# One mLSTM layer on one core: weight buffers of one alignment, SiLU as one function, conv taps on ScalarE, Newton steps on GpSimd

## The chip, the cores and the metric

The kernel runs on one core of a Trainium2 chip. The metric is device time in microseconds (us). Three runs of the kernel before took 1791.73, 1795.51 and 1797.22 us, so the median is 1795.51. PE is the matrix engine (TensorE), DVE is VectorE, ACT is ScalarE, POOL is GpSimd, and SP only issues DMA transfers.

## The reference, cut to what matters

All numbers are float32. There is one layer, with 256 tokens and a width of 4096:

```python
h = rms_norm(x, norm_w)
u = h @ w_in                                  # 4096 -> 2048 q, 2048 k, 4096 v, 4096 og, 4096 z, 16 gates
qk = silu(causal_dwconv(qk, conv_w, conv_b))  # four taps per channel
# for each of 8 heads (q, k of 256, v of 512), tokens in chunks: weights from the gates,
# num = (a * (q @ k.T)) @ v + state terms;  hc = num / max(|qn|, exp(-m))
hn = hc * rsqrt(mean(hc * hc) + EPS) * out_norm_w
y = hn * sigmoid(og) * silu(z)
out = x + y @ w_out
```

## The kernel before

**Products.** Every large product is made of float32 values split into a rounded high half and the rest, the low half (`split`: ACT copies the high half, L135, DVE subtracts to get the low one, L136). `matmul3` then issues three matmuls: high by high, high by low, low by high (L140 to L142). The left operand (128 x 128, activations turned) is the stationary one; a weight block of 128 x 512 moves through.

**Projections.** `project_pair` computes two column blocks of 512 for all 256 tokens. There are 15 pairs over x (`oz0`, `qkv1`, `oz1`, ... `oz7`) and 4 over y (`o0` to `o3`). The 4096 rows are eight chunks. Chunks 0, 2, 4 and 6 (`FAST`) use seven products P1 to P7 in place of eight, for which DVE adds weight blocks (`prepare`, L281: `w<-w,w`); the others use four plain steps. Each step takes one `operand`: a raw weight tile of 2 x 128 rows by 512 columns, kept as 128 x 1024, and its halves `wh` and `wl`. A fast step has 6 matmuls and a plain one 12. A pair has 28 fast and 16 plain steps, so 44 operands and 360 matmuls of 128 x 512; 19 pairs have 6840.

**Buffers.** `wh` and `wl` each rotate over four tiles (tags `whi`, `wlo` of `wpool`) of RAW = 1056 columns, since stage 1 needs that many: 4224 bytes in each partition, 16.5 times 256. So neighbouring tiles start alternately on a multiple of 256 bytes and 128 bytes past one. As 44 is a multiple of 4, a step has the same buffer in every pair. In the built program the four `wh` tiles start at 160640, 164864, 169088 and 173312, the four `wl` tiles follow in the same way; a `wh` tile and its `wl` tile are of one kind, and all left operands start 128 bytes past a multiple of 256.

**Stage 1** (L559 to L604, the first 110 us) needs no normalised x. For each half of a chunk it loads x turned (`xT`) and 1056 + 1024 weight columns (`wf`), scales x by `norm_w` on the fly into the halves `lhs` (L583 on ACT, L584 on DVE), and forms the gates and the q, k, v of head 0 (`first_P`). Beside it `row_squares` and `row_stats` form the rsqrt of each row (`rstd`, `rstdB`), and `build_x` scales x (`xn`, L250) and makes the left operands `lhs_x` of the projections, for chunks 0 to 4 in stage 1 and for 5 to 7 right behind it.

**Heads.** The work of a head sits in a deque, `queue`, of small functions that `pump` runs evenly between the steps of the pairs: `combine` (P1 to P7 out of PSUM), `conv_qk` (turn q or k, ACT's first tap L440, three more taps fused on DVE L447, SiLU as sigmoid L452 and product L453), `head` (weights, `num`, the sum of squares, and `scale`: rsqrt by a seed and three Newton steps on 128 x 2), `gate_1` (sigmoid of og and z, then DVE products L645 and L646), `finish` (y times its rsqrt times the gate, L519) and `turn` (y turned, scaled, spilled to DRAM, L541 and L544). At the end `build_y` loads the spilled chunks and makes `lhs_y`. The tile framework orders the instructions of each engine by a timeline simulation of its own; program order within an engine is then fixed.

```python
hi = wpool.tile([P, RAW], F32R, name=f"wh_{name}", tag="whi")[:, :n]   # L147
for it in range(3):                                                    # L128, rsqrt
    nc.vector.tensor_mul(t, r, r)
    nc.vector.scalar_tensor_tensor(t, t, -0.5, src, op0=OP.mult, op1=OP.mult)
    nc.vector.scalar_tensor_tensor(dst if it == 2 else r, t, 1.5, r, op0=OP.add, op1=OP.mult)
```

Of the kernel before, what the change touches and what calls it, by code (L numbers as in the profile page):

```python
# [11 lines left out]
F32 = mybir.dt.float32  # L12
# [3 lines left out]
OP = mybir.AluOpType  # L16
# [25 lines left out]
FAST = (0, 2, 4, 6)  # L42
# [20 lines left out]
def mlstm_layer(ctx: ExitStack, tc: tile.TileContext, x, xT, norm_w, w_first, w_in, conv_w, conv_b, gate_b,  # L63
# [4 lines left out]
    wpool = ctx.enter_context(tc.tile_pool(name="wpool", bufs=4))  # L68
    work = ctx.enter_context(tc.tile_pool(name="work", bufs=1))
# [51 lines left out]
    def rsqrt(dst, src, n, tag):  # L121

        r = small.tile([P, n], F32, name=f"rs_r_{tag}", tag=f"rs_r{n}", bufs=1)
        t = small.tile([P, n], F32, name=f"rs_t_{tag}", tag=f"rs_t{n}", bufs=1)
        i = small.tile([P, n], I32, name=f"rs_i_{tag}", tag=f"rs_i{n}", bufs=1)
        nc.vector.tensor_scalar(i, src.bitcast(I32), 1, None, op0=OP.logical_shift_right)
        nc.vector.tensor_scalar(r.bitcast(I32), i, -1.0, float(0x5F3759DF), op0=OP.mult, op1=OP.add)
        for it in range(3):  # L128
            nc.vector.tensor_mul(t, r, r)
            nc.vector.scalar_tensor_tensor(t, t, -0.5, src, op0=OP.mult, op1=OP.mult)  # L130
            nc.vector.scalar_tensor_tensor(dst if it == 2 else r, t, 1.5, r, op0=OP.add, op1=OP.mult)
# [12 lines left out]
    def operand(name, src):  # L144

        n = src.shape[-1]
        hi = wpool.tile([P, RAW], F32R, name=f"wh_{name}", tag="whi")[:, :n]  # L147
        lo = wpool.tile([P, RAW], F32R, name=f"wl_{name}", tag="wlo")[:, :n]
        split(hi, lo, src)
        return hi, lo  # L150
# [4 lines left out]
    def load(name, w, off, n):  # L155
        raw = wpool.tile([P, RAW], F32, name=f"w_{name}", tag="wraw", bufs=6)[:, :n]
        nc.sync.dma_start(raw, source(w, off, n))
        return raw
# [37 lines left out]
    def build(c, src, of):  # L196

        if c in FAST:
# [42 lines left out]
    def build_x(c):  # L241
        src = big(f"xn_{c}", [P, CK, T])

        def scaled(j0):
            def run():
                if j0 == 0:
                    nc.sync.dma_start(src, xT[:, c * CK:(c + 1) * CK, :])
                for j in range(j0, j0 + 2):
                    k = c * CK + j
                    nc.vector.scalar_tensor_tensor(src[:, j, :], src[:, j, :], nw[:, k:k + 1], rstdB,  # L250
                                                   op0=OP.mult, op1=OP.mult)
            return run
        return [scaled(0), scaled(2)] + lazy(lambda: build(c, src, "x"), 4 if c in FAST else 2)
# [63 lines left out]
    def project_pair(name, w, off, of, between=None):  # L317
        ps = {}
        plain = [u for c in range(NCH) if c not in FAST for u in plain_steps(name, w, off, c)]
        steps = []  # L320
        for c in FAST:
            for group in fast_steps(name, w, off, c):
                steps += group
                if plain:
                    steps.append(plain.pop(0))
        assert not plain
        uses = {s: len(FAST) * HK for s in TAGS}
        for s in ("P2", "P3", "P4", "P5"):
            uses[s] += (NCH - len(FAST)) * CK
        seen = dict.fromkeys(TAGS, 0)  # L330
        left = {c: 7 if c in FAST else 4 for c in range(NCH)}
# [93 lines left out]
    def conv_qk(h, u):  # L425

        def one(i):
# [27 lines left out]
            return [turned, taps(0), taps(1), silu, lambda: split(qk[i][0], qk[i][1], t_["acc"])]
# [71 lines left out]
    def turn(h):  # L527
# [18 lines left out]
        if h == HEADS - 1:  # L546
            out += lazy(lambda: build(h, yT[0], "y"), 4 if h in FAST else 2)
        return out

    def build_y(c):  # L550
# [5 lines left out]
        return [make] + lazy(lambda: build(c, src[0], "y"), 4 if c in FAST else 2)  # L556
# [4 lines left out]
    FW = GQ + DQK + DV  # L561
    for c in range(NCH):
# [4 lines left out]
        for k0 in range(0, CK, HK):  # L567
            parts = [(0, 1), (1, 2)] if c == 0 and k0 == 0 else [(0, HK)]
            for a, z in parts:
# [36 lines left out]

    u0 = work.tile([P, NT, NB], F32, name="u_0", tag="cA")
# [9 lines left out]
    hs, finish = head(0)  # L617
# [6 lines left out]
    for n, (what, h, _, _) in enumerate(pairs):  # L624
# [7 lines left out]
        if what == "qkv":  # L632
            hs, finish = head(h)
# [41 lines left out]
def blocks_of(w, s1, s2):  # L675
# [3 lines left out]
    for c in range(NCH):  # L679
        if c in FAST:  # L680
# [36 lines left out]
```

## Time and profile before

| | us |
|---|---|
| three runs, median | 1795.51 |
| the profiled execution, its own time | 1793.31 |
| its span in the profile | 1791.6 |
| PE busy | 1756.1 (98%) |
| DVE busy | 1655.5 (92%) |
| ACT busy | 1107.1 (62%) |
| POOL busy | 12.1 (1%) |

The granted clock of PE is 0.993 of full speed over the whole span. A page shows busy time by engine, what each engine waited for, and groups of instructions by source line. An engine that is busy most of the time need not be the one that ends last; the waits tell that. Matmuls overlap in the array: one lasts about 0.39 us in the profile, and the next starts some 0.23 us after it, so for PE the distance of starts counts and not the duration.

### The profile page before, as it was taken

What the parts mean: (1) busy time and instruction counts of PE and PEld (TensorE: products, weight loads), DVE (VectorE), ACT (ScalarE), POOL (GpSimd) and SP (SyncE); (2) the same over time, 40 slices, a digit from 0 to 9 for tenths busy, and PEclk for the clock granted to TensorE, in tenths of its full rate; (3) what the DMA queues carried; (4) which work ended last, traced back from release to release, by engine and by line L of the source; (5) the groups of instructions that cost most, each with busy time, mean ns of one, the idle gap of its engine ahead of it and who ended that gap; (6) DMA issues with size and microseconds to landing.
All of it is one profiled execution on the core that took longest, in us unless ns stands there. A gap on an engine that the chain in (4) does not pass through costs nothing.

```text
span 1791.6 us, 21695 instructions
## 1 busy us (share of the span) xinstructions
PE 1756.1 (98%) x7804; PEld 1419.5 (79%) x7804; DVE 1655.5 (92%) x1823; ACT 1107.1 (62%) x1271; POOL 12.1 (1%) x29
## 2 busy tenths in 40 slices
PE   9979999999999999999999999999999989999998
PEld 8867878888888788788878887888788768787876
DVE  5899999999999999989998999899999999989897
ACT  7566666665666666656666566566656666565654
POOL 0000000000000000000000000000000000000000
PEclk9999999999999999999999999999999989999999
DMA  9755565556555656565556566655555747767563
GB/s 368 262 167 193 171 221 191 193 190 219 192 192 179 217 182 202 174 234 188 188 192 218 188 193 205 208 186 195 202 193 183 234 154 258 244 212 241 195 221 121
DMA packets 107724, 365.67 MB, mean 204 GB/s; under 512 B 12128, under 2 KB 12512, under 8 KB 107616
## 3 DMA queue, kind: packets, MB, share of 16 engines
q1 hardware_dynamic: 105360, 356.95, 59.4%
q0 software_dynamic: 1968, 6.82, 1.0%
q8 instruction: 61, 1.00, 0.2%
q10 hardware_dynamic: 288, 0.52, 0.1%
q14 instruction: 47, 0.39, 0.1%
HBM read 356.38 MB, written 7.86 MB: 203 GB/s over the span
## 4 chain that ended last, share of the span: by engine, by line
PE 86%; DVE 7%; ACT 3%; issue 2%; DMA 1%; SPq 0%; DVEq 0%; ACTq 0%
PE P_oz L140 11%; PE P_oz L141 11%; PE P_oz L142 11%; PE P_qkv L141 10%; PE P_qkv L142 10%; PE P_qkv L140 10%; PE P_o L141 5%; PE P_o L142 5%; PE P_o L140 5%; ACT wh_qkv_P L135 1%; PE first_P L140 1%; PE first_P L141 1%; PE first_P L142 1%; DVE wl_oz_P L136 1%; DVE wl_oz L136 1%
## 5 line engine op out<-in xcount | busy, mean ns | idle before, releaser
L135 ACT ACTIVATE wh_oz_P<-w_oz 128x1024 fp32r<-128x1024 f32 x224 | 233.8, 1056 | 166.2 <-DVE w_oz L281 85.7
L136 DVE TENSOR_TENSOR wl_oz_P<-w_oz,wh_oz_P 128x1024 fp32r<-128x1024 f32 x224 | 269.0, 1216 | 19.5 <-ACT wh_oz_P L135 19.5
L135 ACT ACTIVATE wh_qkv_P<-w_qkv 128x1024 fp32r<-128x1024 f32 x196 | 206.4, 1060 | 114.3 <-PE P_qkv L142 77.6
L136 DVE TENSOR_TENSOR wl_qkv_P<-w_qkv,wh_qkv_P 128x1024 fp32r<-128x1024 f32 x196 | 236.8, 1220 | 29.8 <-ACT wh_qkv_P L135 28.7
L141 PE MATMUL P_oz<-wl_oz,lhs_x 128*128 128x512 f32 x512 | 202.7, 396 | 0.0
L142 PE MATMUL P_oz<-wh_oz,lhs_x 128*128 128x512 f32 x512 | 201.3, 393 | 0.0
L140 PE MATMUL P_oz<-wh_oz,lhs_x 128*128 128x512 f32 x512 | 195.2, 396 | 1.8 <-ACT wh_oz L135 0.9
L141 PE MATMUL P_oz<-wl_oz_P,lhs_x 128*128 128x512 f32 x448 | 179.0, 400 | 1.1 <-DVE wl_oz_P L136 1.1
L140 PE MATMUL P_oz<-wh_oz_P,lhs_x 128*128 128x512 f32 x448 | 175.9, 402 | 3.9 <-ACT wh_oz_P L135 3.8
L141 PE MATMUL P_qkv<-wl_qkv,lhs_x 128*128 128x512 f32 x448 | 177.4, 396 | 0.9 <-DVE wl_qkv L136 0.9
L142 PE MATMUL P_oz<-wh_oz_P,lhs_x 128*128 128x512 f32 x448 | 177.1, 395 | 0.0
L142 PE MATMUL P_qkv<-wh_qkv,lhs_x 128*128 128x512 f32 x448 | 176.1, 393 | 0.0
L135 ACT ACTIVATE wh_o_P<-w_o 128x1024 fp32r<-128x1024 f32 x112 | 117.6, 1059 | 93.5 <-PE P_o L142 53.1
L135 ACT ACTIVATE wh_qkv<-w_qkv 128x1024 fp32r<-128x1024 f32 x112 | 118.5, 1058 | 79.2 <-PE P_qkv L142 66.0
L140 PE MATMUL P_qkv<-wh_qkv,lhs_x 128*128 128x512 f32 x448 | 166.7, 393 | 0.0
L135 ACT ACTIVATE wh_oz<-w_oz 128x1024 fp32r<-128x1024 f32 x128 | 134.8, 1053 | 47.4 <-PE P_oz L142 22.5
L136 DVE TENSOR_TENSOR wl_oz<-w_oz,wh_oz 128x1024 fp32r<-128x1024 f32 x128 | 155.7, 1217 | 7.5 <-ACT wh_oz L135 7.3
L281 DVE TENSOR_TENSOR w_oz<-w_oz,w_oz 128x1024 f32<-128x1024 f32 x128 | 155.7, 1217 | 0.5
L141 PE MATMUL P_qkv<-wl_qkv_P,lhs_x 128*128 128x512 f32 x392 | 154.7, 395 | 0.0
L142 PE MATMUL P_qkv<-wh_qkv_P,lhs_x 128*128 128x512 f32 x392 | 154.2, 393 | 0.0
L136 DVE TENSOR_TENSOR wl_o_P<-w_o,wh_o_P 128x1024 fp32r<-128x1024 f32 x112 | 135.3, 1219 | 18.9 <-ACT wh_o_P L135 18.8
L140 PE MATMUL P_qkv<-wh_qkv_P,lhs_x 128*128 128x512 f32 x392 | 150.2, 398 | 1.1 <-ACT wh_qkv_P L135 1.0
(216 smaller groups left out, 3436.7 us busy)
## 6 DMA issues: line engine op xcount, KB each, us to landing
w_oz<-in_w_in SPq DMA_DIRECT2D x256, 512.0 KB, 4.3
w_qkv<-in_w_in SPq DMA_DIRECT2D x224, 512.0 KB, 4.3
w_o<-in_w_out SPq DMA_DIRECT2D x128, 512.0 KB, 4.4
wf<-in_w_first SPq DMA_DIRECT2D x15, 528.0 KB, 6.7
wf<-in_w_first SPq DMA_DIRECT2D x15, 512.0 KB, 6.7
xr<-in_x SPq DMA_DIRECT2D x8, 512.0 KB, 8.6
xn<-in_xT SPq DMA_DIRECT2D x8, 512.0 KB, 5.7
xo<-in_x SPq DMA_DIRECT2D x16, 256.0 KB, 5.2
```

What stands on the lines that cost most here:

```text
L135: nc.scalar.activation(hi, src, AF.Copy)
L136: nc.vector.tensor_sub(lo, src, hi.bitcast(F32))
L140: nc.tensor.matmul(ps, a[0], b[0], start=first, stop=False)
L141: nc.tensor.matmul(ps, a[0], b[1], start=False, stop=False)
L142: nc.tensor.matmul(ps, a[1], b[0], start=False, stop=last)
L281: nc.vector.tensor_add(raw[step[1]], raw[step[1]], raw[step[2]])
```

## The change

1. The `wh` and `wl` tiles have 1024 columns (4096 bytes), so all of them start at the same offset; in the built program this is 128 bytes past a multiple of 4096. Raw weights get a pool of their own (still 1056 columns). The 1056-column operands of stage 1 go to `wide_operand`: two pairs of work tiles, `v0`/`v1` and `cA`/`cB`, in turn. `V` moves to the tags `v0`/`v1`.
2. SiLU is one ACT function (`AF.Silu`), for the convolution and for z; the DVE product behind the sigmoid is gone. ACT loads its function tables 27 times in place of 19: `gate_1` now has two loads.
3. A tap of the convolution is a scaled copy on ACT for each of two blocks and one DVE addition over both.
4. A Newton step of `rsqrt` has four plain operations in place of three, two of them fused. The one of a head runs on GpSimd (with `ss`), except the two integer operations of its seed. The one of the rows stays on DVE.
5. `build_x`: four scalings by `norm_w` on ACT, then one DVE product of 128 x 1024 with `rstdB`.
6. Stage 1: x is scaled in place on ACT, and both blocks of a half chunk are split in one operation of 128 x 512 on each engine.
7. `FAST` becomes a dictionary with the same chunks for x and y; the plain steps are dealt out by a formula that gives the same order as before.

Instructions on each engine, before and after: DVE 1767 and 1618, ACT 1191 and 1273, POOL 34 and 138; PE and SP are equal.

```diff
-FAST = (0, 2, 4, 6)
+FAST = {"x": (0, 2, 4, 6), "y": (0, 2, 4, 6)}
     wpool = ctx.enter_context(tc.tile_pool(name="wpool", bufs=4))
+    rawpool = ctx.enter_context(tc.tile_pool(name="rawpool", bufs=6))
-    def rsqrt(dst, src, n, tag):
+    def rsqrt(dst, src, n, tag, eng=nc.vector):
...
-            nc.vector.tensor_mul(t, r, r)
-            nc.vector.scalar_tensor_tensor(t, t, -0.5, src, op0=OP.mult, op1=OP.mult)
-            nc.vector.scalar_tensor_tensor(dst if it == 2 else r, t, 1.5, r, op0=OP.add, op1=OP.mult)
+            eng.tensor_mul(t, r, r)
+            eng.tensor_mul(t, t, src)
+            eng.tensor_scalar(t, t, -0.5, 1.5, op0=OP.mult, op1=OP.add)
+            eng.tensor_mul(dst if it == 2 else r, t, r)

...
     def operand(name, src):

         n = src.shape[-1]
-        hi = wpool.tile([P, RAW], F32R, name=f"wh_{name}", tag="whi")[:, :n]
-        lo = wpool.tile([P, RAW], F32R, name=f"wl_{name}", tag="wlo")[:, :n]
+        hi = wpool.tile([P, HK * NB], F32R, name=f"wh_{name}", tag="whi")[:, :n]
+        lo = wpool.tile([P, HK * NB], F32R, name=f"wl_{name}", tag="wlo")[:, :n]
         split(hi, lo, src)
         return hi, lo

+    def wide_operand(name, src, n):
+
+        tags = (("v0", "v1"), ("cA", "cB"))[n % 2]
+        hi, lo = (work.tile([P, RAW], F32R, name=f"w{i}_{name}", tag=tag)[:, :src.shape[-1]]
+                  for i, tag in enumerate(tags))
+        split(hi, lo, src)
+        return hi, lo
+
     def source(w, off, n):
         return bass.AP(tensor=w.tensor, offset=w.offset + off, ap=[[n, P], [1, n]])

     def load(name, w, off, n):
-        raw = wpool.tile([P, RAW], F32, name=f"w_{name}", tag="wraw", bufs=6)[:, :n]
+        raw = rawpool.tile([P, RAW], F32, name=f"w_{name}", tag="wraw")[:, :n]
         nc.sync.dma_start(raw, source(w, off, n))
         return raw

...
     def build_x(c):
         src = big(f"xn_{c}", [P, CK, T])

-        def scaled(j0):
-            def run():
-                if j0 == 0:
-                    nc.sync.dma_start(src, xT[:, c * CK:(c + 1) * CK, :])
-                for j in range(j0, j0 + 2):
-                    k = c * CK + j
-                    nc.vector.scalar_tensor_tensor(src[:, j, :], src[:, j, :], nw[:, k:k + 1], rstdB,
-                                                   op0=OP.mult, op1=OP.mult)
-            return run
-        return [scaled(0), scaled(2)] + lazy(lambda: build(c, src, "x"), 4 if c in FAST else 2)
+        def scaled():
+            nc.sync.dma_start(src, xT[:, c * CK:(c + 1) * CK, :])
+            for j in range(CK):
+                nc.scalar.activation(src[:, j, :], src[:, j, :], AF.Copy, scale=nw[:, c * CK + j:c * CK + j + 1])
+            nc.vector.tensor_mul(src, src, rstdB.unsqueeze(1).to_broadcast([P, CK, T]))
...
         ps = {}
-        plain = [u for c in range(NCH) if c not in FAST for u in plain_steps(name, w, off, c)]
+        fast = FAST[of]
...
-                t_["acc"], t_["sg"] = both[:, 0], both[:, 1]
+                t_["acc"], t_["tp"] = both[:, 0], both[:, 1]
...
-            def taps(a):
+            def tap(j):
                 def run():
-                    acc, pt, ct = t_["acc"], t_["pt"], ct0 + a
-                    for j in range(1, CONV):
-                        nc.vector.scalar_tensor_tensor(acc[:, a, j:], pt[:, a, :T - j], cw[:, 3 - j, ct:ct + 1],
-                                                       acc[:, a, j:], op0=OP.mult, op1=OP.add)
+                    acc, tp, pt = t_["acc"], t_["tp"], t_["pt"]
+                    for a in range(2):
+                        nc.scalar.activation(tp[:, a, :T - j], pt[:, a, :T - j], AF.Copy,
+                                             scale=cw[:, 3 - j, ct0 + a:ct0 + a + 1])
+                    nc.vector.tensor_add(acc[:, :, j:], acc[:, :, j:], tp[:, :, :T - j])
                 return run

             def silu():
-                nc.scalar.activation(t_["sg"], t_["acc"], AF.Sigmoid)
-                nc.vector.tensor_mul(t_["acc"], t_["acc"], t_["sg"])
-
-            return [turned, taps(0), taps(1), silu, lambda: split(qk[i][0], qk[i][1], t_["acc"])]
+                nc.scalar.activation(t_["acc"], t_["acc"], AF.Silu)
+
+            return [turned, tap(1), tap(2), tap(3), silu, lambda: split(qk[i][0], qk[i][1], t_["acc"])]
         return one(0) + one(1)


-    V = [lhs_pool.tile([P, NT, DV], F32R, name=f"v{part}") for part in range(2)]
     y = {}

-    def head(h):
+    def head(h, V):

         qT, kT = qk
         A = [work.tile([P, 3 * P], F32R, name=f"A{part}_{h}", tag=f"A{part}") for part in range(2)]
...
         def scale():
-            nc.vector.tensor_scalar(ss, ss, 1.0 / DV, EPS, op0=OP.mult, op1=OP.add)
-            rsqrt(s2, ss, NT, f"h{h}")
+            nc.gpsimd.tensor_scalar(ss, ss, 1.0 / DV, EPS, op0=OP.mult, op1=OP.add)
+            rsqrt(s2, ss, NT, f"h{h}", nc.gpsimd)
...
                     ws.append(raw)
                 for k in range(k0 + a, k0 + z):
-                    s = nw[:, c * CK + k:c * CK + k + 1]
-                    nc.scalar.activation(xh[:, k, :], xraw[:, k, :], AF.Copy, scale=s)
-                    nc.vector.scalar_tensor_tensor(xl[:, k, :], xraw[:, k, :], s, xh[:, k, :].bitcast(F32),
-                                                   op0=OP.mult, op1=OP.subtract)
-                ops = [operand(f"f_{c}_{k0}_{a}_{i}", raw) for i, raw in enumerate(ws)]
+                    nc.scalar.activation(xraw[:, k, :], xraw[:, k, :], AF.Copy, scale=nw[:, c * CK + k:c * CK + k + 1])
+                split(xh[:, k0 + a:k0 + z, :], xl[:, k0 + a:k0 + z, :], xraw[:, k0 + a:k0 + z, :])
+                ops = [wide_operand(f"f_{c}_{k0}_{a}", ws[0], wides), operand(f"f_{c}_{k0}_{a}", ws[1])]
+                wides += 1
                 for k in range(n):
                     kk = k0 + a + k
                     for i, (o, wd, b) in enumerate(first):
...

+    V = [work.tile([P, RAW], F32R, name=f"v{part}", tag=f"v{part}")[:, :NT * DV].rearrange("p (t c) -> p t c", t=NT)
+         for part in range(2)]
     u0 = work.tile([P, NT, NB], F32, name="u_0", tag="cA")
...
         else:
-            sg = {}
-
-            def gate_1(A=A, B=B, sg=sg):
-
-                sg[0] = big("sg", [P, NT, NB])
+            def gate_1(A=A, B=B):
+
                 nc.scalar.activation(A, A, AF.Sigmoid)
-                nc.scalar.activation(sg[0], B, AF.Sigmoid)
-
-            todo += [gate_1, lambda B=B, sg=sg: nc.vector.tensor_mul(B, B, sg[0]),
-                     lambda A=A, B=B: nc.vector.tensor_mul(B, B, A)]
+                nc.scalar.activation(B, B, AF.Silu)
+
+            todo += [gate_1, lambda A=A, B=B: nc.vector.tensor_mul(B, B, A)]
             todo += finish(B) + turn(h)
         queue.extendleft(reversed(todo))

```

Where the order moves. On ACT in stage 1, around the scaling of chunk 6 (`lhs_6`; `xn` and `lhs_x` belong to `build_x`, `wf` are stage 1's weights), before:

```order
L135 ACTIVATE wh_f_2_0_1_819<-wf_2_0_1_809 128x1024
L135 ACTIVATE lhs_x_865<-F_x_866 128x512
L583 ACTIVATE lhs_6_875<-xT_874,nw 128x256 x4
L135 ACTIVATE wh_f_0_0_0_885<-wf_0_0_0_877 128x1056
L135 ACTIVATE wh_f_0_0_1_889<-wf_0_0_1_879 128x1024
```

and of the change:

```order
L137 ACTIVATE lhs_x_873<-F_x_874 128x512
L586 ACTIVATE xT_882<-xT_882,nw 128x256 x4
L257 ACTIVATE xn_990<-xn_990,nw 128x256 x4
L137 ACTIVATE lhs_6_883<-xT_882 128x512
L137 ACTIVATE w_f_0_0_893<-wf_0_0_0_885 128x1056
L137 ACTIVATE lhs_6_883<-xT_882 128x512
L137 ACTIVATE wh_f_0_0_1040<-wf_0_0_1_1030 128x1024
```

The high half of the left operand came out of the scaling itself; now four scalings of `xT`, and four of the x of `build_x`, stand ahead of the first copy that makes it.

On ACT, the gate of head 1 among the weight halves of the pair `qkv2` that follows it (rows are named by step: `1_2` is plain step 2 of chunk 1), before:

```order
L135 ACTIVATE wh_qkv_1_2_3502<-w_qkv_1_2_3500 128x1024
L642 ACT_TABLE_LOAD
L642 ACTIVATE A_oz_3368<-A_oz_3368 128x1024
L643 ACTIVATE sg<-B_oz_3369 128x1024
L135 ACTIVATE wh_qkv_0_P_3520<-w_qkv_0_21_3471 128x1024
```

and of the change:

```order
L137 ACTIVATE wh_qkv_1_2_3529<-w_qkv_1_2_3527 128x1024
L644 ACT_TABLE_LOAD
L644 ACTIVATE A_oz_3396<-A_oz_3396 128x1024
L645 ACT_TABLE_LOAD
L645 ACTIVATE B_oz_3397<-B_oz_3397 128x1024
L137 ACTIVATE wh_qkv_0_P_3547<-w_qkv_0_21_3499 128x1024
```

The gate stands at the same place; between its two functions there is a second table load.

On DVE, the rsqrt of head 1 (`rs_i_h` and `rs_r_h` are the seed, `ss` the sum of squares), before:

```order
L514 TENSOR_SCALAR ss_2633<-ss_2633 128x2
L126 TENSOR_SCALAR rs_i_h_3105<-ss_2633 128x2
L127 TENSOR_SCALAR rs_r_h_3103<-rs_i_h_3105 128x2
L129 TENSOR_TENSOR rs_t_h_3104<-rs_r_h_3103 128x2
L130 SCALAR_TENSOR_TENSOR rs_t_h_3104<-rs_t_h_3104,ss_2633 128x2
L131 SCALAR_TENSOR_TENSOR rs_r_h_3103<-rs_t_h_3104,rs_r_h_3103 128x2
L136 TENSOR_TENSOR wl_oz_6_P_3312<-w_oz_6_21_3299,wh_oz_6_P_3311 128x1024
L129 TENSOR_TENSOR rs_t_h_3104<-rs_r_h_3103 128x2
```

Of the change, on POOL, whose rows from here to the next head's are these steps and the spill alone:

```order
L517 TENSOR_SCALAR ss_2654<-ss_2654 128x2
L130 TENSOR_TENSOR rs_t_h_3157<-rs_r_h_3156 128x2
L131 TENSOR_TENSOR rs_t_h_3157<-rs_t_h_3157,ss_2654 128x2
L132 TENSOR_SCALAR rs_t_h_3157<-rs_t_h_3157 128x2
L133 TENSOR_TENSOR rs_r_h_3156<-rs_t_h_3157,rs_r_h_3156 128x2
...
L133 TENSOR_TENSOR s_1_2655<-rs_t_h_3157,rs_r_h_3156 128x2
L547 DMA spill_3625<-yT_3592 128x1024
```

The Newton steps left DVE, where the two operations of the seed stay; its reader, y's scaling by `s_1`, is still on DVE, some 30 instructions behind the seed.

## Rows read from the trace of the kernel before

**Rows 1.** The page, busy us, share of the span, instructions.

```profile
PE 1756.1 (98%) x7804; PEld 1419.5 (79%) x7804; DVE 1655.5 (92%) x1823; ACT 1107.1 (62%) x1271; POOL 12.1 (1%) x29
```

**Rows 2.** Waits of PE: us in total, times, longest us.

```profile
PE first_P L140 <- ACT lhs L583: 7.3, 3, 3.4
PE P_o L140 <- ACT wh_o_P L135: 4.7, 9, 2.2
```

**Rows 3.** Windows: length, busy us (instructions) by engine, granted clock, DMA share, GB/s.

```profile
110.00:150.00 40.00, 34.22 (x136) 25.48 (x136) 40.00 (x56) 25.71 (x35) 0.00 (x0) 0.96 0.42 137
300.00:400.00 100.00, 100.00 (x446) 81.15 (x445) 94.92 (x114) 65.29 (x77) 0.00 (x0) 1.00 0.58 190
1420.00:1480.00 60.00, 52.32 (x187) 38.29 (x186) 59.93 (x84) 37.20 (x48) 0.00 (x0) 0.89 0.53 176
1500.00:1600.00 100.00, 99.38 (x429) 80.23 (x428) 91.06 (x83) 57.85 (x58) 2.17 (x4) 1.00 0.66 223
```

**Rows 4.** Timeline of PE (start, duration), weight buffer on a multiple of 256 bytes.

```profile
1742.72 0.62 PE L140 MATMUL P_o<-wh_o,lhs_y 128*128 128x512 f32 x2
...
1745.51 0.39 PE L140 MATMUL P_o<-wh_o_P,lhs_y 128*128 128x512 f32 x1
```

**Rows 5.** Timeline of PE, weight buffer 128 bytes past a multiple of 256.

```profile
1763.48 0.63 PE L140 MATMUL P_o<-wh_o,lhs_y 128*128 128x512 f32 x2
...
1766.23 0.40 PE L140 MATMUL P_o<-wh_o_P,lhs_y 128*128 128x512 f32 x1
```

**Rows 6.** Timeline of DVE behind stage 1.

```profile
140.26 1.21 DVE L281 TENSOR_TENSOR w_oz<-w_oz,w_oz 128x1024 f32<-128x1024 f32 x1
141.40 0.46 DVE L447 SCALAR_TENSOR_TENSOR acc<-pt,cw,acc 128x253 f32<-128x253 f32 x1
141.79 1.20 DVE L281 TENSOR_TENSOR w_oz<-w_oz,w_oz 128x1024 f32<-128x1024 f32 x1
```

**Rows 7.** Groups of DVE by line: busy us, mean ns, idle before.

```profile
L453 DVE TENSOR_TENSOR acc<-acc 128x512 f32<-128x512 f32 x16 | 10.9, 682 | 0.0
```

**Rows 8.** Timeline of ACT in stage 1, at PE's second wait.

```profile
57.01 1.71 ACT L583 ACTIVATE lhs<-xT,nw 128x256 fp32r<-128x256 f32 x4 [1.21 <-DMA xT<-in_xT]
```

**Rows 9.** Timeline of PE in stage 1, at its second and third wait.

```profile
57.57 0.40 PE L140 MATMUL first_P<-wh_f,lhs 128*128 128x272 f32 x1 [2.43 <-ACT lhs L583]
57.98 0.43 PE L140 MATMUL first_P<-wh_f,lhs 128*128 128x272 f32 x1
...
96.96 0.39 PE L140 MATMUL first_P<-wh_f,lhs 128*128 128x272 f32 x1 [3.36 <-ACT lhs L583]
...
97.31 0.30 PE L140 MATMUL first_P<-wh_f,lhs 128*128 128x272 f32 x1
```

**Rows 10.** Groups of ACT by line: busy us, mean ns, idle before.

```profile
L541 ACT ACTIVATE yT<-py,onw 128x256 f32<-128x256 f32 x32 | 13.3, 471 | 30.8 <-PE py L537 30.8
L135 ACT ACTIVATE lhs_x<-xn 128x512 fp32r<-128x512 f32 x12 | 7.1, 621 | 9.5 <-DVE xn L250 9.5
```

**Rows 11.** Timeline of ACT at the gate of head 1.

```profile
394.91 1.28 ACT L642 ACT_TABLE_LOAD   x1
396.21 1.06 ACT L642 ACTIVATE A_oz<-A_oz 128x1024 f32<-128x1024 f32 x1
397.18 1.04 ACT L643 ACTIVATE sg<-B_oz 128x1024 f32<-128x1024 f32 x1
```

**Rows 12.** Timeline of DVE in head 1: seed, last Newton step, y's scaling.

```profile
370.07 0.17 DVE L127 TENSOR_SCALAR rs_r_h<-rs_i_h 128x2 int32<-128x2 int32 x1
...
378.32 0.15 DVE L131 SCALAR_TENSOR_TENSOR s<-rs_t_h,rs_r_h 128x2 f32<-128x2 f32 x1
...
403.94 1.41 DVE L519 SCALAR_TENSOR_TENSOR y<-y,s,B_oz 128x512 f32<-128x512 f32 x2
```

**Rows 13.** Groups of POOL by line: its arithmetic at the start.

```profile
L92 POOL TENSOR_SCALAR_AFFINE_SELECT tri<-tri 128x128 f32<-128x128 f32 x1 | 0.3, 287 | 0.0
L709 POOL MEMSET const-float32-1.0<- 128x1 f32 x1 | 0.1, 98 | 0.0
```

More of the change, by code (lines that the diff above doesn't have):

```diff
@@ L196, in build @@
     def build(c, src, of):
-        if c in FAST:
+        if c in FAST[of]:
             flat = lhs_pool.tile([P, 2 * 7 * HK * P], F32R, name=f"lhs_{of}_{c}", tag=f"lhs{c}")
@@ L242, in build_x @@
         src = big(f"xn_{c}", [P, CK, T])
-        def scaled(j0):
-            def run():
-                if j0 == 0:
-                    nc.sync.dma_start(src, xT[:, c * CK:(c + 1) * CK, :])
-                for j in range(j0, j0 + 2):
-                    k = c * CK + j
-                    nc.vector.scalar_tensor_tensor(src[:, j, :], src[:, j, :], nw[:, k:k + 1], rstdB,
-                                                   op0=OP.mult, op1=OP.mult)
-            return run
-        return [scaled(0), scaled(2)] + lazy(lambda: build(c, src, "x"), 4 if c in FAST else 2)
+        def scaled():
[3 more added lines that the diff above has]
+            nc.vector.tensor_mul(src, src, rstdB.unsqueeze(1).to_broadcast([P, CK, T]))
+        return [scaled] + lazy(lambda: build(c, src, "x"), 4 if c in FAST["x"] else 2)
     def lazy(make, n):
@@ L318, in project_pair @@
         ps = {}
-        plain = [u for c in range(NCH) if c not in FAST for u in plain_steps(name, w, off, c)]
+        fast = FAST[of]
+        plain = [u for c in range(NCH) if c not in fast for u in plain_steps(name, w, off, c)]
+        groups = [g for c in fast for g in fast_steps(name, w, off, c)]
         steps = []
[L321 to L327, printed above, removed]
+        for i, group in enumerate(groups):
+            steps += group + plain[i * len(plain) // len(groups):(i + 1) * len(plain) // len(groups)]
+        uses = {s: len(fast) * HK for s in TAGS}
         for s in ("P2", "P3", "P4", "P5"):
-            uses[s] += (NCH - len(FAST)) * CK
+            uses[s] += (NCH - len(fast)) * CK
         seen = dict.fromkeys(TAGS, 0)
-        left = {c: 7 if c in FAST else 4 for c in range(NCH)}
+        left = {c: 7 if c in fast else 4 for c in range(NCH)}
         for n, (c, make, cost) in enumerate(steps):
@@ L546, in turn @@
         if h == HEADS - 1:
-            out += lazy(lambda: build(h, yT[0], "y"), 4 if h in FAST else 2)
+            out += lazy(lambda: build(h, yT[0], "y"), 4 if h in FAST["y"] else 2)
         return out
@@ L555, in make @@
             nc.sync.dma_start(src[0], spill[c])
-        return [make] + lazy(lambda: build(c, src[0], "y"), 4 if c in FAST else 2)
+        return [make] + lazy(lambda: build(c, src[0], "y"), 4 if c in FAST["y"] else 2)
     banks = [bank(f"first_{s}", s) for s in TAGS[:6]]
@@ L561, in mlstm_layer @@
     FW = GQ + DQK + DV
+    wides = 0
     for c in range(NCH):
@@ L574, in mlstm_layer @@
                     wd = hi_c - lo_c
-                    raw = wpool.tile([P, RAW], F32, name=f"wf_{c}_{k0}_{a}_{i}", tag="wraw", bufs=6)[:, :n * wd]
+                    raw = rawpool.tile([P, RAW], F32, name=f"wf_{c}_{k0}_{a}_{i}", tag="wraw")[:, :n * wd]
                     nc.sync.dma_start(raw.rearrange("p (k n) -> p k n", k=n),
@@ L616, in mlstm_layer @@
                                        op0=OP.mult, op1=OP.subtract)
-    hs, finish = head(0)
+    hs, finish = head(0, V)
     for c in range(5, NCH):
@@ L632, in mlstm_layer @@
         if what == "qkv":
-            hs, finish = head(h)
+            hs, finish = head(h, V)
             todo += [lambda t=t, B=B: split(V[0][:, t, :], V[1][:, t, :], B[:, t, :]) for t in range(NT)]
@@ L672, in mlstm_layer, with blocks_of @@
         pump()
-def blocks_of(w, s1, s2):
+def blocks_of(w, s1, s2, of):
     n1, n2 = (np.concatenate([w[:, a:a + n] for a, n in s], axis=1).reshape(NCH, 2, HK, P, NB) for s in (s1, s2))
@@ L679, in blocks_of @@
     for c in range(NCH):
-        if c in FAST:
+        if c in FAST[of]:
             b = (n1[c, 0], n2[c, 0], n2[c, 1], n1[c, 1])
@@ L701 @@
                                         .reshape(KT, P, -1).transpose(1, 0, 2)).reshape(-1),
-        "w_in": np.concatenate([blocks_of(w_in, s1, s2) for _, _, s1, s2 in block_pairs()]),
+        "w_in": np.concatenate([blocks_of(w_in, s1, s2, "x") for _, _, s1, s2 in block_pairs()]),
         "conv_w": np.ascontiguousarray(inputs["a_conv_w"][0].reshape(CONV, 2 * QK // P, P).transpose(2, 0, 1)),
@@ L706 @@
         "out_norm_w": np.ascontiguousarray(inputs["a_out_norm_w"][0].reshape(KT, P).T),
-        "w_out": np.concatenate([blocks_of(w_out, [(a, NB)], [(a + NB, NB)]) for a in range(0, D, 2 * NB)]),
+        "w_out": np.concatenate([blocks_of(w_out, [(a, NB)], [(a + NB, NB)], "y") for a in range(0, D, 2 * NB)]),
     }
```

## The prediction

> **What bounds the kernel now.** I read the busy times on the page first: PE 98%, DVE 92%, ACT 62%, GpSimd next to nothing [rows 1]. PE sets the end, so the question is what its time is made of. Then the waits of PE: the largest are 7.3 us in three waits of stage 1 for the left operand that ACT makes and 4.7 us at the output projection [rows 2]; all its waits together are about 26 us of 1791.6. The rest is 6,840 projection matmuls (19 pairs of column blocks by 360). So there are two places to win or lose: the interval between matmuls and the stretches where PE waits. The windows show the second [rows 3]: at 300 to 400 us DVE is busy 95% and PE 100%, so DVE, though nearly full, holds nobody up; at 110 to 150 and 1420 to 1480 DVE is full to the last 0.1 us and PE loses 5.8 and 7.7 us, the second at a granted clock of 0.89 of full speed. DVE's work is worth its time in those two stretches and nothing in the others.
>
> The first needs the start times of PE. A step's matmuls read one pair of weight buffers. Out of a buffer that starts on a multiple of 256 bytes, twelve take 2.79 us from first to thirteenth start [rows 4], 232.5 ns each; out of one that starts 128 bytes off, 2.75 us [rows 5], 229 ns. These two are examples: by the start times of the whole trace, with each buffer's place from the built program, the stretches of eleven or more from one buffer are at 232.6 ns on a multiple of 256 bytes (97 stretches) and at 229.0 ns otherwise (90). Over all 512-column projection matmuls, with the borders between buffers, it is 232.3 against 229.9 ns. Four buffers go round and a pair has 44 operands, so half of the matmuls are of either kind.
>
> **The change, part by part.**
>
> Alignment. The buffers become 4,096 instead of 4,224 bytes, and all start 128 bytes past a multiple of 4,096: the quicker class. If the interval belongs to the buffer's place, 231.1 ns becomes 229.9, and 6,840 x 1.2 ns = 8.2 us go. The bounds: 0, if it belongs to something else that differs between the four buffers, and 6,840 x 2.1 = 14.4 us, if 229.0 is reached over the borders too. I take 8.2, since 229.9 is also what the second kind shows with its borders.
>
> DVE at the start (110 to 150 us). An operation costs DVE its distance to the next start: 1.14 us for 128x1024, 0.39 for a tap [rows 6]. Four chunks of x lose four fused scalings (4 x 0.39 = 1.6 us by that distance) for one product of 1.14: -1.9. Head 0's q convolution has six taps (2.3) that become three additions of 128x2x255 (nearest row: 128x512, 0.68 long, about 0.60 apart [rows 7]): -0.5. The SiLU product goes: -0.6. Sum -3.0, and -3.2 with head 0's small Newton steps that leave DVE; all on the path, as DVE is full there. The bounds: 0, if ACT, which takes the scalings and taps, is late in DVE's place, and -5.8, all that PE loses there.
>
> ACT in stage 1. Now ACT scales and rounds 128x256 in one operation and the first matmul goes 0.56 us after it starts: ACT at 57.01, PE at 57.57; the third wait ends in the same way at 96.96 [rows 8, 9]. After the change ACT first scales two or four blocks in place (1.71 us for four [rows 8]), then copies 128x512 (0.62 [rows 10]), so the first matmul comes 0.56 + 1.8 later if a wait is for these. At three places, 5.4 us; 0, if the transfer comes earlier or ACT finds its turn before the earlier chunk's matmuls end. I take half, +3.0, as the three waits are for the transfer itself and the order of ACT has moved.
>
> The x to y transition (1420 to 1480). DVE loses one 128x1024 product (1.14 between starts) and about ten small Newton steps of 0.15 [rows 12]: -2.6, taken as -2.7. Down to -5 if the clock stays up; nothing, if ACT is last there: [rows 2] names ACT, but behind a full DVE.
>
> Steady state: ACT. Per head, six fused taps on each of two turns go to ACT as scaled copies out of PSUM, twelve in all (0.47 each [rows 10]): 5.7 us, and one table load of 1.28 more [rows 11]. ACT is at 65 us of 100 [rows 3], so the total is covered. What counts is the longest block: the gate takes 1.28 + 1.06 + 1.04 = 3.4 us now and 2 x 1.28 + 2 x 1.06 = 4.7 us after, and in it no weight half is made. Ahead of PE stand up to four buffer pairs, each worth 6 or 12 matmuls, 8.2 on average: 4 x 8.2 x 0.231 = 7.6 us, and 5.5 if all are short. I take 0; if only two pairs are filled at that time the block is 0.9 us too long in 8 heads: +7. In the trace the operation behind the load starts 1.30 us after the load does, just when it ends [rows 11]. The Trainium skill (ScalarE: Activation LUTs, "What ACT_TABLE_LOAD costs") puts a drain beside the load, about 2.7 us in all; by it the block would be 7.4 us, just inside the cover. The trace doesn't show the drain, so the sum goes without it.
>
> Steady state: GpSimd. The twelve Newton steps of a head move to GpSimd. Its only arithmetic in the trace is at the start: 0.10 us for a memset of 128x1, 0.29 for a select over 128x128 [rows 13]. No row shows it beside DVE. From 0.1 to 0.3 each it is 1.2 to 3.5 us; if every step waits out a DVE instruction of 1.22, 13 x 1.5 = 20 us. What is behind it: y's scaling on DVE, in whose queue the low halves wait. Between the seed and y's scaling lie 33.9 us now (370.07 to 403.94 [rows 12]); afterwards some 30 DVE instructions in heads 1 to 6, some 55 in head 7, and only about ten, some 12 us, in head 0. I take 0 for all; the upper bound is head 0 late by 20 - 12 = 8 us, of which the buffers hide 7.6. The row stays on DVE with three more steps of 0.15: +0.5, left in the rounding.
>
> DVE's weight additions and low halves read two SBUF tiles each: 304 and 836 of them by 1.22 us are 78% of the span. The Trainium skill (SBUF — State Buffer, "SBUF: two separate sides") says that such a VectorE operation and a GpSimd operation that reads SBUF exclude each other for a whole instruction, and the loser blocks. No row of this trace shows it; it gives the third rival its mechanism.
>
> The project pair's new dictionary changes neither the count nor the order of steps.
>
> Sum on the profiled execution (span 1791.6, its own time 1793.3): 1793.3 - 8.2 - 3.2 + 3.0 - 2.7 = 1782.2. That execution lies 2.2 us below the median of the runs; I say 1783.
>
> **The rivals.**
> 1. The interval doesn't follow the alignment (0.18). The four buffers also differ in distance to other data, and the new ones share one offset, hi with lo. Against: the slowest of the 90 stretches has 231.3, the quickest of the 97 has 231.4, and each class has two of the four pairs. Then 1783 + 8 = 1791.
> 2. ACT is late in stage 1 (0.12): all three waits grow by 1.8, and PE, idle longer, falls to half clock after each, as after the second wait already: the same matmul takes 0.43 at 57.98 and 0.30 at 97.31 [rows 9]. For 10 us at half speed it loses 5: 1783 + 2.4 + 5 + 3 (no gain at the start) = 1793.
> 3. Slower: GpSimd starves (0.07). If each of its steps waits for three DVE instructions of 1.22, a chain takes 12 x 3.7 = 44 us. It decides when a step takes over (33.9 + 7.6)/12 = 3.5 us. Six heads are then 2.5 us late and head 0 44 - 12 - 7.6 = 24: 1783 + 39 = 1822. For it: DVE is at 95%. Against: DVE waits often for ACT, and the steps are tiny.
> 4. More (0.11): 229.0 ns over all borders and both transitions without loss of clock: 1783 - 6.2 - 2.3 - 6 = 1768 or so.
>
> **How the numbers follow.** The forecast has 0.52, rivals 0.18, 0.12, 0.07 and 0.11. Its own range is 1776 to 1791: the start and the transition each 3 us either way, ACT in stage 1 from 0 to 5.4. A measurement of this kernel can tell about 0.3%, 5.4 us: faster is below 1790.1, slower above 1800.9. Faster: 0.47 of the forecast, 0.09 of the first rival, all of the fourth: 0.67. Slower: the third, and 0.05 of the first two where the gate or head 0 costs as well: 0.12. Same: 0.21. The range for 8 in 10 runs from 1768 (the fourth rival's middle) to 1798 (the second with the gate block's cost): 1768 to 1798.
>
> **What would show it.** Alignment: the same steps' matmuls at 229 to 230 ns, at all four buffers; if half of them stay at 232.5, or all go there, the first term is wrong. DVE: about 50 us less busy, seen in PE in the two stretches alone; in 110 to 150 and 1420 to 1480 PE's loss down by 3 each. ACT: 8 more table loads, some 80 us more busy; a wait of PE for a high half right behind the gate's second load would refute the cover. Stage 1: the waits of first_P longer than 7.3 us in sum by about 3. GpSimd: y's scaling on DVE doesn't wait for it; a wait there, head 0's first, is the third rival. The forecast is wrong altogether if the interval of the matmuls in steady state is still 231 ns.

## The result and the profile after

The changed kernel takes 1770.51 us (median of 4 runs, 1768.7 to 1771.52) against 1795.09 for the kernel before: a ratio of 0.9864, interval [0.9846, 0.9881]. That is faster by 24.6 us, inside the range for 8 in 10 (1768 to 1798) but below the forecast's own range (1776 to 1791), and twice the 12 us forecast. The profiled execution takes 1768.70 us with a span of 1767.0.

The page's busy times after, answering to [rows 1]:

```profile
PE 1726.2 (98%) x7804; PEld 1418.0 (80%) x7804; DVE 1614.0 (91%) x1635; ACT 1174.6 (66%) x1424; POOL 96.4 (5%) x133
```

PE has as many instructions as before and 30 us less busy time; ACT has 67.5 us more, where some 80 were forecast, and DVE 41.5 less, where 50 were. By the pages DVE has 188 instructions fewer and ACT 153 more, not the 149 and 82 that the counts given with the change come to.

The waits of PE after (us in total, times, longest), to [rows 2]:

```profile
PE first_P L142 <- ACT lhs L137: 7.6, 3, 4.2
PE P_o L142 <- ACT wh_o_P L137: 4.2, 9, 1.6
PE P_oz L142 <- ACT wh_oz_P L137: 3.3, 4, 1.3
...
PE P_qkv L142 <- ACT wh_qkv L137: 2.7, 6, 0.4
...
PE P_qkv L142 <- ACT wh_qkv_P L137: 1.7, 6, 0.3
```

The waits did not shrink: all waits of PE together are 32.1 us, against 26.5 before. So the gain lies in the interval between matmuls. The same two steps of the last pair as in [rows 4, 5] show it, as starts and durations on PE after:

```profile
1718.83 0.62 PE L142 MATMUL P_o<-wh_o,lhs_y 128*128 128x512 f32 x2
...
1721.55 0.39 PE L142 MATMUL P_o<-wh_o_P,lhs_y 128*128 128x512 f32 x1
...
1739.23 0.62 PE L142 MATMUL P_o<-wh_o,lhs_y 128*128 128x512 f32 x2
...
1741.95 0.39 PE L142 MATMUL P_o<-wh_o_P,lhs_y 128*128 128x512 f32 x1
```

Twelve take 2.72 us in both, 226.7 ns each, against 232.5 [rows 4] and 229 [rows 5]. Over all projection matmuls with no wait between them (intervals under 260 ns; all means below are taken in this way) the mean fell from 231.1 to 227.2 ns: 6840 x 3.9 = 26.7 us, where the forecast has 8.2.

Cut at counts of the projection matmuls, the time went so (us; one profile each, so a difference of about 1 us says little):

| kernel | first one starts | 1 to 181 | 181 to 5221 | to 5581 (transition) | to the last |
|---|---|---|---|---|---|
| before | 108.5 | 53.7 | 1219.3 | 106.8 | 294.5 |
| changed | 108.5 | 49.8 | 1204.0 | 105.4 | 290.4 |
| e1 place only | 108.9 | 49.6 | 1205.6 | 107.6 | 290.4 |
| e9 wide only | 110.0 | 49.2 | 1217.0 | 106.8 | 294.6 |
| e2 old place | 110.0 | 49.8 | 1220.4 | 104.6 | 294.1 |
| e10 no wide | 115.0 | 50.5 | 1222.4 | 107.4 | 294.5 |

Steady state (181 to 5221) alone gives 15.3 us and the output projections at the end 4.1. In each of the two PE had waited for less than 2 us before, so a relief of DVE cannot explain them.

### The profile page after: what moved, and what is told of

The parts are those of the page before. It is cut to its first block, busy times and chain, and to the rows that moved or that the text cites. A ratio compares the mean times of both kernels' runs of the same rounds, so it can differ in the third digit from the quotient of the medians.

```text
span 1767.0 us, 21802 instructions
## 1 busy us (share of the span) xinstructions
PE 1726.2 (98%) x7804; PEld 1418.0 (80%) x7804; DVE 1614.0 (91%) x1635; ACT 1174.6 (66%) x1424; POOL 96.4 (5%) x133
## 4 chain that ended last, share of the span: by engine, by line
PE 85%; DVE 7%; ACT 4%; issue 2%; DMA 2%; SPq 0%; POOL 0%; DVEq 0%; ACTq 0%
PE P_oz L143 11%; PE P_oz L142 11%; PE P_oz L144 11%; PE P_qkv L143 11%; PE P_qkv L142 10%; PE P_qkv L144 10%; PE P_o L142 5%; PE P_o L143 5%; PE P_o L144 5%; PE first_P L142 1%; DVE wl_o_P L138 1%; PE first_P L143 1%; PE first_P L144 1%; DMA wf<-in_w_first 1%; DVE w_o L287 1%
## 5 line engine op out<-in xcount | busy, mean ns | idle before, releaser
L142 PE MATMUL P_oz<-wh_oz_P,lhs_x 128*128 128x512 f32 x448 | 173.2, 393 | 3.8 <-ACT wh_oz_P L137 3.3
L144 PE MATMUL P_oz<-wh_oz_P,lhs_x 128*128 128x512 f32 x448 | 175.0, 391 | 0.0
L137 ACT ACTIVATE wh_oz<-w_oz 128x1024 fp32r<-128x1024 f32 x128 | 135.2, 1056 | 49.6 <-PE P_oz L144 23.4
L144 PE MATMUL P_qkv<-wh_qkv_P,lhs_x 128*128 128x512 f32 x392 | 152.6, 389 | 0.0
L142 PE MATMUL P_qkv<-wh_qkv_P,lhs_x 128*128 128x512 f32 x392 | 147.2, 392 | 1.7 <-ACT wh_qkv_P L137 1.7
```

What stands on the lines that cost most here:

```text
L137: nc.scalar.activation(hi, src, AF.Copy)
L142: nc.tensor.matmul(ps, a[0], b[0], start=first, stop=False)
L144: nc.tensor.matmul(ps, a[1], b[0], start=False, stop=last)
```

## The experiments

Each ratio is to the kernel before on the same chip; the number in ns is the mean interval of the projection matmuls.

**e1: the place of the buffers alone**, in the kernel before, with the tiles that it needs.

```diff
-        hi = wpool.tile([P, RAW], F32R, name=f"wh_{name}", tag="whi")[:, :n]
+        hi = wpool.tile([P, HK * NB], F32R, name=f"wh_{name}", tag="whi")[:, :n]
...
+                ops = [wide_operand(f"f_{c}_{k0}_{a}", ws[0], wides), operand(f"f_{c}_{k0}_{a}", ws[1])]
```

> The kernel before with only the new places of the weight buffers (and what that needs: a pool for raw weights, wide operands of stage 1 and V elsewhere). Theory A (the whole gain is the buffers' place; the second kind's 229.9 ns of before was pulled up by the neighbours of the first kind): projection matmuls at about 227.3 ns in steady state, 1795 - 6840 x 3.9 ns = 1768.5 us. Theory B (the forecast's size: place gives 8 us, the rest of the gain comes from the relief of DVE): 1787 us at 229.9 ns.

1773.41 us, ratio 0.988 [0.9865, 0.9895], 227.3 ns. The interval is the one of theory A, the time is 4.9 us above its 1768.5. Edit 1 alone, with the wide operands' own tiles, is worth 21.9 us, close to the 24.6 of the whole change; e9 below takes the two apart.

**e2: the place undone**, everything else as changed.

```diff
-        hi = wpool.tile([P, HK * NB], F32R, name=f"wh_{name}", tag="whi")[:, :n]
+        hi = wpool.tile([P, RAW], F32R, name=f"wh_{name}", tag="whi")[:, :n]
```

> The changed kernel with weight buffers of 4224 bytes again, everything else as changed. Theory A: back to 231 ns, 1770.5 + 26.6 = 1797 us, so that the other edits together give nothing (3 us won at the start, 5 lost behind the gates). Theory B: 1770.5 + 8 = 1779 us.

1789.84 us, 0.9973 [0.9962, 0.9984], 230.7 ns. Between the two: the place is worth 19.3 us here, and 5.5 us come from all the rest, the wide operands of edit 1 included. Theory B is out in both.

**e3 and e4: which place.** 128 unused bytes ahead of the weight buffers, or ahead of everything.

```diff
     wpool = ctx.enter_context(tc.tile_pool(name="wpool", bufs=4))
+    wpool.tile([P, 32], F32, name="pad", tag="pad", bufs=1)
```

> The changed kernel with 128 unused bytes ahead of the weight buffers: all eight start on a multiple of 256 bytes, the left operands stay 128 bytes past one. Theory P (the place itself counts): 233.3 ns, as in the long stretches from such buffers before, 1770.5 + 6840 x 6.1 ns = 1812 us, slower than the kernel before. Theory U (only the switch between two kinds costs, any one place is quick): 227 ns, 1770 us. Theory R (the distance of weights and left operand modulo 256 counts): 1812 us as P.

```diff
     const = ctx.enter_context(tc.tile_pool(name="const", bufs=1))
+    const.tile([P, 32], F32, name="pad")
```

> The changed kernel with 128 unused bytes ahead of everything: left operands and weight buffers all start on a multiple of 256 bytes, their distance is that of the changed kernel. Theory P (place of the weights): 233 ns, 1812 us. Theory R (distance to the left operand): 227 ns, 1770 us. Theory U: 1770 us.

e3: 1804.05 us, 1.0048 [1.0033, 1.0063], slower than before, at 232.8 ns; its size is below the 1812 expected. e4: 1770.06 us, 0.9857 [0.9841, 0.9874], at 227.2 ns. The first of the two steps above, on PE in e3 and then in e4:

```profile
1753.54 0.63 PE L143 MATMUL P_o<-wh_o,lhs_y 128*128 128x512 f32 x2
...
1756.33 0.39 PE L143 MATMUL P_o<-wh_o_P,lhs_y 128*128 128x512 f32 x1
```

```profile
1722.68 0.61 PE L143 MATMUL P_o<-wh_o,lhs_y 128*128 128x512 f32 x2
...
1725.40 0.39 PE L143 MATMUL P_o<-wh_o_P,lhs_y 128*128 128x512 f32 x1
```

2.79 and 2.72 us with weights at the same kind of address, a multiple of 256 bytes. So the place itself (P) is refuted by e4 and its uniformity (U) by e3: what counts is the distance between the moving operand and the stationary one (R). In e3 the tiles behind the weights move with them, in e4 everything moves; of what stays in place in e3 alone, the projection matmuls read only the left operands.

**e5: a distance of 64 bytes.** As e3, with a pad of 16 columns.

> The changed kernel with 64 unused bytes ahead of the weight buffers: they start 192 bytes past a multiple of 256, the left operands 128. Theory R256 (weights and left operand must stand a multiple of 256 bytes apart): slow, 232.8 ns as at a distance of 128, 1804 us. Theory R7 (only whether both lie in the same half of 256 bytes counts): 227.2 ns, 1770 us. A value between the two would mean that the loss grows with the distance.

1783.01 us, 0.9943 [0.9928, 0.9958], 229.2 ns. The step takes 2.75 us:

```profile
1733.01 0.62 PE L143 MATMUL P_o<-wh_o,lhs_y 128*128 128x512 f32 x2
...
1735.76 0.39 PE L143 MATMUL P_o<-wh_o_P,lhs_y 128*128 128x512 f32 x1
```

Neither extreme: 227.2, 229.2 and 232.8 ns at distances of 0, 64 and 128 bytes. This fits a loss that grows with the distance; no other distance was run.

**e9 and e10: the rest of edit 1.** e9 is e1 with buffers of 4224 bytes; e10 is e2 with stage 1's wide operands in the four shared buffers again.

```diff
-                ops = [wide_operand(f"f_{c}_{k0}_{a}", ws[0], wides), operand(f"f_{c}_{k0}_{a}", ws[1])]
-                wides += 1
+                ops = [operand(f"f_{c}_{k0}_{a}_{i}", raw) for i, raw in enumerate(ws)]
```

> The kernel before with stage 1's wide operands, V and the raw weights in their new tiles, but weight buffers of 4224 bytes, and none of the other edits. Theory W (the 4 us at the start of the projections come from this: the four buffers are free earlier when stage 1 ends): the first 180 projection matmuls in 49.8 us in place of 53.7, 1795 - 4 = 1791 us. Theory S (they come from DVE's relief or from the place): 53.7 us, 1795 us.

> The changed kernel with edit 1 undone (weight buffers of 4224 bytes, which stage 1's wide operands share again; V keeps its new tiles): the relief of DVE alone. Theory D (the relief wins the start by itself, as the forecast says): the first 180 projection matmuls in about 50 us, total 1795 - 3 - 2.5 (transition) + 4.5 (gates) = 1794 us. Theory W (only the wide operands' own tiles win it): 53 us and 1797 us.

e9: 1789.0 us, 0.9974 [0.9965, 0.9984]; the first 180 take 49.2 us: theory W holds. Between e9 and e1 only the place differs: 21.9 - 4.7 = 17.2 us in this kernel. e10: 1799.9 us, 1.003 [1.002, 1.0039], slower than before; its first 180 take 50.5, the number of theory D. But they start 6.5 us later than before, when DVE has had more time to work ahead, and they end 3.3 us later (165.6 against 162.2), so a gain from DVE's relief is not shown by it. With the wide operands in their own tiles the relief adds nothing to this stretch (49.2 without it in e9, 49.8 with it in e2). Where e10 loses, the waits of PE say in part:

```profile
PE first_P L142 <- ACT lhs L137: 10.9, 4, 4.5
```

10.9 us in place of 7.3 [rows 2], and the first projection matmul starts at 115.0 in place of 108.5: the wait is for ACT, which has more to do in stage 1. With the wide operands in their own tiles most of this is gone (e2 starts at 110.0; other profiles of kernels with both edits range from 108.5 to 112.6).

**e7: Newton steps on DVE again.**

```diff
-            nc.gpsimd.tensor_scalar(ss, ss, 1.0 / DV, EPS, op0=OP.mult, op1=OP.add)
-            rsqrt(s2, ss, NT, f"h{h}", nc.gpsimd)
+            nc.vector.tensor_scalar(ss, ss, 1.0 / DV, EPS, op0=OP.mult, op1=OP.add)
+            rsqrt(s2, ss, NT, f"h{h}")
```

> The changed kernel with the heads' Newton steps (and the scaling of the sum of squares) on DVE again, in the new form of four operations. Theory N (on GpSimd they cost nothing and save DVE, which has room outside the two full stretches, nothing that counts): 1770.5 us, within 1.5. Theory L (GpSimd's steps hold DVE up, as their 0.4 to 1.0 us each may mean): quicker, by up to 8 heads x 12 x 0.3 = 29 us.

1773.01 us, 0.9889 [0.9874, 0.9904], 2.5 us above the changed kernel, with an interval that overlaps its own: no difference is shown. The gain of theory L is not there, so it is out.

**e8 and e11: the table loads.** e8 has the gate as before, e11 the convolution's SiLU as well (19 loads).

```diff
-                nc.scalar.activation(B, B, AF.Silu)
+                nc.scalar.activation(sg[0], B, AF.Sigmoid)
...
+            todo += [gate_1, lambda B=B, sg=sg: nc.vector.tensor_mul(B, B, sg[0]),
```

```diff
-                nc.scalar.activation(t_["acc"], t_["acc"], AF.Silu)
+                nc.scalar.activation(t_["tp"], t_["acc"], AF.Sigmoid)
+                nc.vector.tensor_mul(t_["acc"], t_["acc"], t_["tp"])
```

> The changed kernel with the gate as before: both functions are sigmoid, one table load, and a DVE product with z. Theory T (PE's two short waits behind the gate's second table load cost 0.6 to 0.7 us in each of seven heads): 1770.5 - 4.5 = 1766 us, and these waits gone. Theory D (DVE's extra product of 1.22 us per head costs as much): 1770 us.

> The changed kernel with every SiLU as sigmoid and DVE product: 19 table loads in place of 27, 2.6 us more on DVE for each head. Theory T (PE's waits behind table loads cost 4.4 us over the heads, and with the gate's sigmoid alone the load only moved to the convolution): 1770.5 - 4.4 = 1766 us. Theory D (DVE's work costs more than the loads): 1770 us or more.

e8: 1774.57 us, 0.9901 [0.9884, 0.9917], which is slower than the changed kernel by 4.1 us, against both theories. The wait on `wh_qkv` behind the gate is gone, but in the pairs `oz` PE now waits 10.1 us for ACT, where the changed kernel has 3.3:

```profile
PE P_oz L142 <- ACT wh_oz_P L137: 10.1, 11, 1.6
```

The kernel still has 26 loads: the convolution's SiLU now needs one of its own, and there the cover is thinner: seven heads have a wait of 0.94 to 0.96 us behind it. 4.5 us lie between the ends of two high halves there, and PE starts 15 matmuls in them. e11: 1769.27 us, 0.9855 [0.9841, 0.987]: both waits are gone, and PE's waits in steady state fall from 6.2 to 2.1 us. But steady state takes 1202.9 us against 1204.0, and no difference in the sum can be told; where the other 3 us went is not shown.

**e12 and e13: all places, and both.** e12 starts the tiles of stage 1's wide operands and of V at the distance 0 as well (the blocks of 256 and 272 columns inside the wide ones still begin 0, 64 or 128 bytes past it), e13 is e11 and e12 together, as a candidate.

```diff
-        hi, lo = (work.tile([P, RAW], F32R, name=f"w{i}_{name}", tag=tag)[:, :src.shape[-1]]
+        hi, lo = (work.tile([P, RAW + 32], F32R, name=f"w{i}_{name}", tag=tag)[:, :src.shape[-1]]
```

> The changed kernel with 128 more bytes in the tiles of stage 1's wide operands and of V, so that all of them also stand a multiple of 256 bytes from the left operands: half of them did not. If the law of the distance holds for these too: matmuls of the lo half in stage 1 and of num quicker, some 1 to 3 us, 1768 us; if stage 1 is bound by its transfers, only num: 1770 us.

> The last two together, as a candidate to beat both kernels. If their gains add: 1764 us; if neither gives anything, 1770 us.

1770.84 us, 0.9864 [0.9849, 0.9878], and 1768.78 us, 0.9855 [0.9839, 0.9872]. Neither can be told from the changed kernel; e13 has the lowest median, but the gains do not add to the 1764 us hoped for.

## Why the prediction was wrong in size

**The alignment: the step that failed.** I took 8.2 us for it, from 229.9 ns, "since 229.9 is also what the second kind shows with its borders", and 14.4 us, from 229.0 ns, as the utmost. Both were means over matmuls that still suffered from the first kind (weights on a multiple of 256 bytes), whose buffers take turns with the second. In the 90 stretches of the second kind, the first five intervals average 231.2 ns, from the tenth on they are 227.0 or less; the stretches are hardly longer than that. The row was there: the seventh start of [rows 5] is followed by six intervals of 226.7 ns on average, up to the last row of that group. It is this one, of the kernel before:

```profile
1764.87 0.39 PE L142 MATMUL P_o<-wh_o,lhs_y 128*128 128x512 f32 x1
```

When all buffers are of one kind, no matmul pays for the switch: 227.2 ns. The term is 24 to 27 us by the intervals (230.7 in e2, 231.1 before) and 17.2 to 19.3 by the time (e9 against e1, e2 against the changed kernel). Part of the difference goes into waits: those of PE grow from 23.7 to 32.1 us between e9 and e1, and from 29.5 to 32.1 between e2 and the changed kernel. The direction of the step was right; its reason, an address 128 bytes past a multiple of 256, was not. By e3 and e4 it is the distance to the left operand, which in the kernel before, with all left operands on one place, looked the same.

**An edit without a term.** I described the wide operands and priced them at nothing. They leave the four buffers free before stage 1 ends: ACT starts the first high half for the projections at 86.7 us in e9, at 102.6 before. They win 4.7 us by themselves (e9), and 10.1 with ACT's added work (e2 against e10).

**DVE at the start, -3.2:** e10 has 50.5 in place of 53.7, the same 3.2 us. As its stretch starts and ends later than before, this agreement may be luck. The wide operands win the same stretch, and there the relief of DVE adds nothing (e9, e2).

**ACT in stage 1, +3.0:** by the start of the first projection matmul it is +6.5 without the wide operands (e10) and 0 to 4 with them. The waits of `first_P` are 7.6 us in the changed kernel, not 3 longer. ACT is late as described; that the wide operands take most of it back was overlooked.

**The transition, -2.7:** e2 against e9 104.6 and 106.8, the changed kernel against e1 105.4 and 107.6: -2.2 both times. Without the wide operands it is not seen: 107.4 in e10, 106.8 before.

**The gate, 0:** it costs, and by the sign that the forecast names: PE waits for a high half right behind the second load. ACT at the gate of a later head, and PE behind it:

```profile
902.29 1.07 ACT L137 ACTIVATE wh_qkv<-w_qkv 128x1024 fp32r<-128x1024 f32 x1 [1.66 <-PE P_qkv L144]
903.38 1.28 ACT L644 ACT_TABLE_LOAD   x1
904.67 1.06 ACT L644 ACTIVATE A_oz<-A_oz 128x1024 f32<-128x1024 f32 x1
905.75 1.28 ACT L645 ACT_TABLE_LOAD   x1
907.05 1.06 ACT L645 ACTIVATE B_oz<-B_oz 128x1024 f32<-128x1024 f32 x1
908.01 1.04 ACT L137 ACTIVATE wh_qkv_P<-w_qkv 128x1024 fp32r<-128x1024 f32 x1
```

```profile
909.11 0.50 PE L142 MATMUL P_qkv<-wh_qkv_P,lhs_x 128*128 128x512 f32 x1 [0.28 <-ACT wh_qkv_P L137]
910.06 0.49 PE L142 MATMUL P_qkv<-wh_qkv,lhs_x 128*128 128x512 f32 x1 [0.45 <-ACT wh_qkv L137]
```

The block is 4.63 us from load to the start of the next high half, as worked out, with no drain behind a load. But PE needs this half finished: from the end of the last one (903.36) to the end of the next (909.05) it is 5.7 us. The cover was smaller than 7.6 us, too. The four pairs were taken, as ACT had waited 1.66 us until PE let one go (first row above), but in these 5.7 us PE starts 23 matmuls, 5.2 us, and not four times 8.2: this is close to the forecast's 5.5, "if all are short". So there are two waits of 0.28 and 0.45 us, in six heads (1.7 and 2.7 us in total). The forecast's other case, "if only two pairs are filled", did not happen, and its 7 us are more than the 4.4 of these waits. Taking the load away at the gate alone moves it to the convolution (e8); taking all away wins nothing that can be told (e11).

**GpSimd, 0:** right, though a step takes up to six times as long beside DVE. GpSimd in head 1, and DVE beside it:

```profile
362.70 0.20 POOL L130 TENSOR_TENSOR rs_t_h<-rs_r_h 128x2 f32<-128x2 f32 x1 [0.56 <-DVE rs_r_h L128]
362.97 1.15 POOL L131 TENSOR_TENSOR rs_t_h<-rs_t_h,ss 128x2 f32<-128x2 f32 x1
364.20 0.19 POOL L132 TENSOR_SCALAR rs_t_h<-rs_t_h 128x2 f32<-128x2 f32 x1
...
373.39 1.18 POOL L133 TENSOR_TENSOR s<-rs_t_h,rs_r_h 128x2 f32<-128x2 f32 x1
```

```profile
362.17 0.17 DVE L127 TENSOR_SCALAR rs_i_h<-ss 128x2 int32<-128x2 int32 x1 [2.64 <-POOL ss L517]
...
362.84 1.23 DVE L138 TENSOR_TENSOR wl_oz_P<-w_oz,wh_oz_P 128x1024 fp32r<-128x1024 f32 x1 [0.29 <-ACT wh_oz_P L137]
```

An operation on 128x2 lasts 0.19 us where DVE waits and 1.15 where DVE has a two-input operation of 1.23: it ends just as DVE's does (364.12 and 364.07). The Trainium skill (SBUF — State Buffer, "SBUF: two separate sides") says that two such operations exclude each other for a whole instruction; the trace agrees. The seed on DVE now waits 2.64 us (the row above), mostly for the sum of squares that ACT makes: with the steps on DVE (e7) the same six waits are 14.1 us in all, against 15.8. PE has no wait around it. The chain from 361.95 to 374.57 is 12.6 us, between my 3.5 and 20, and far from the 41.5 at which the third rival would decide.

**The rivals.** The fourth (more, 1768) came nearest in its number, in part by luck: the interval fell below its 229.0, but the transitions gained no more than the forecast says, and in 1420 to 1480 the granted clock is 0.92, not full. The first is refuted by e1, though the "distance to other data" that it names is what e3 and e4 showed to count. The third is refuted by GpSimd's rows; that ACT is late, as in the second, is in e10.

**Two slips in the sums.** Four times (1.6 - 1.14) is 1.8 and not 1.9, and 1782.2 with the 2.2 us between that execution and the median is 1784, not 1783. Neither matters beside the 12 us that were missed.

Not settled: why the interval grows with the distance, and why a switch of kind takes some nine matmuls to fade. The distance is shown for moving blocks of 512 columns alone: those of 256 and 272 columns in stage 1 of the changed kernel, at 0, 64, 128 and 192 bytes, follow each other at 116 to 119 and 124 to 127 ns, in no order of distance.

## What to carry to other kernels

Where PE is the bound, look at the intervals of matmuls buffer by buffer before the waits: a pool's tile size that is no multiple of 256 bytes put half of the moving operands at the wrong distance from the stationary ones, and cost 17 to 19 us, where all waits of PE came to 26.5. A mean over the better of two mixed kinds is no bound for a kernel that has only that kind; read the best stretch far from the last switch. When an edit moves buffers, price whom the freed ones serve, and price two edits that win the same stretch once.

## What the runs showed of the hardware

Float32 matmuls of 128x512 follow each other at 227.2, 229.2 and 232.8 ns when moving and stationary operand stand 0, 64 and 128 bytes apart modulo 256, at a granted clock of 0.99 of full speed. At 128 the intervals alternate, about 237 and 229 ns in the kernel before. In head 1 of the changed kernel a GpSimd operation on 128x2 takes 0.18 to 0.20 us by itself and 1.04 to 1.19 beside a two-input DVE operation on 128x1024. On ACT the function behind a table load starts 1.29 us after the load starts, in all 27 of them.
